# Splitting a vector multiplication, and replanning the first products, in a fast matrix-multiplication kernel

## The chip, the core and the metric

The kernel runs on one core of one Trainium2 chip. The metric is the time on the device in microseconds, as the median of several runs. Five engines matter here: PE (TensorE, the matrix multiplier) with its weight loads, DVE (VectorE), ACT (ScalarE), POOL (GpSimd) and SP (SyncE). POOL and SP mainly issue transfers (DMA) here.

## The reference

```python
x:  16 x 512 x 1024 float32     w1, w2: 1024 x 768 float32
y1 = np.matmul(x, w1)
y2 = np.matmul(x, w2)
return (np.tanh(y1) * y2).astype(np.float32)
```

So 8192 rows of x are multiplied with 1536 columns, and the two halves of the result are joined row by row.

## The kernel before

**Rows and columns.** The rows are cut into 64 row tiles of 128. The contraction length 1024 is cut into 8 blocks of 128 (`KO`), in two halves of four (`KH`). The 1536 columns are cut into three blocks of 512: block a is columns 0 to 511 of w1, block b is columns 0 to 511 of w2, and block g holds the last 256 columns of both. So `tanh(a) * b` gives the first 512 output columns of a row tile (`o`, 128x768), and one half of g times the tanh of the other half gives the last 256.

**Plain part.** The first four row tiles (`HEAD`) are multiplied directly, slice by slice as the weights land: a slices, then g slices, then b slices (lines 420 to 434).

**Triples.** The other 60 row tiles are worked through in 20 triples of three row tiles. A triple is a product of a 3x2 block matrix (three row tiles by two halves of the contraction) with a 2x3 one (two halves by a, b, g). Eighteen block products would be needed; a Strassen-like scheme does it with 15, called p0 to p14 in the list `C_OPS`. Each is four matmuls of 128x512 into one of the 8 PSUM banks (line 443). For it VectorE forms sums of transposed x blocks (`A_SUMS`, named S3, S15 and so on, line 411) and once sums of weight blocks (`B_SUMS`, named B5, B27 and so on, line 402). The products are put together by copies on ScalarE (line 447), which also seed banks that PE then adds to, and by additions on VectorE (line 453; add4, add60 and so on). A triple ends with a tanh on ScalarE for each row tile and column part (line 456; `t` for 512 columns, `th` for 256) and a multiplication on VectorE (line 461; `m` for 512 columns, `mh` for 256). In names like `p6.0` below, the number behind the point is the triple. p6 multiplies the x sum S15, p1 the sum S3, p0 reads the weight sum B27.

**Getting x in.** Row tiles 4, 5 and 6 (the first triple, loaded in the order 6, 4, 5) come by DMA from POOL (line 352), are transposed by PE (line 370), and are evacuated by ScalarE (line 356). Later row tiles are loaded the same way and transposed by DMA from SP (line 377). The b slices are loaded from POOL (line 349), behind one instruction, `gate` (line 483), that waits for the cast of slice g0; the x rows follow them.

**The order.** Nothing runs in an order chosen on the chip: a planner in the kernel's Python (`Planner`) simulates the five engines with given costs, landing times and due times, and writes out the order in which every engine executes. PE's products have a fixed sequence (`PE_ORDER`, with `FIRST_ORDER` for triple 0 and `LAST_ORDER` for the last triple). What the planner gives out is an order alone; on the chip every instruction waits for what it needs, in its place in its engine's queue. So a changed cost or landing time in the plan changes which instruction stands ahead of which, and which bank it uses.

The assumed landings of the first loads (`lands`) grow by a fixed step for each load, and from `LAG_FROM` on all are put later by `LAG`. The casts from float32 to float16 of the a slices are planned on VectorE, those of the g slices on ScalarE (`CAST`).

Row tile 3 has its b part multiplied at the very end, as fillers of 256 columns between the last products (`FILLERS`).

Of the kernel before, what the change touches and what calls it, by code (L numbers as in the profile page):

```python
# [66 lines left out]
)  # L67

PE_ORDER = "7 0+ 13+ 6 10 4+ 5+ 9 12 1 14 3+ 2+ 11 8"
FIRST_ORDER = "10 7 1 6 12 9 11 14 8"  # L70
LAST_ORDER = "0 5 4 13 14 3 2"
FILLERS = "p0", "p3"

# [1 line left out]
class Planner:  # L75
# [9 lines left out]
    def op(self, name, engines, due, needs, fn, *args, behind=(), issued=(), chains=(), xfer=0.0, latency=None, seeds=False,  # L85
           lands=None, hold=0.0):
        assert name not in self.ops, name
        self.ops[name] = dict(engines=engines, due=due, needs=[n for n in needs if n], behind=[n for n in behind if n], issued=[n for n in issued if n], fn=fn, args=args,
                              chains=chains, xfer=xfer, latency=latency, seeds=seeds, lands=lands, hold=hold)
        for c in chains:  # L90
            self.chains.setdefault(c, {"left": 0, "bank": None, "end": 0.0, "act": 0.0, "dve": 0.0})["left"] += 1
# [135 lines left out]
def kernel(  # L227
# [15 lines left out]
    G = N - F  # L243
    HEAD = 4
    TRIPLES = (MT - HEAD) // 3
# [58 lines left out]
    op = plan.op  # L304
# [179 lines left out]

    MM = 0.2158
    SLOT = KH * MM
    CAST = {"a": {"dve": 0.37}, "g": {"act": 0.495}}
    FINE = (5, 36, 37, 45)
    START = 28.6
    ORIGIN = START - 6 * SLOT  # L490
# [2 lines left out]
    for n, entry in enumerate(PE_ORDER.split()):  # L493
        for i in range(TRIPLES):
            position["p" + entry.rstrip("+"), i] = (i + (entry[-1] == "+")) * 15 + n
    for n, p in enumerate(FIRST_ORDER.split()):
        position["p" + p, 0] = 6 + n
# [4 lines left out]
    plan.strict = [f"{p}.{i}" for _, i, p in sequence]  # L502

    XX = 1.4
    LAG_FROM, LAG = 23.0, 1.2
    on_sp = "x00 x10 x20 x30 x01 x11 a4 a5 x21 a6 x31 a7".split() + [f"g{k}{t}" for k in range(KH) for t in range(2)]
    late = [f"b{k}" for s, k in slices if s == "b"]
    rows_in = (HEAD + 2, HEAD, HEAD + 1)
# [11 lines left out]
    for n, what in enumerate(on_sp):  # L520
# [3 lines left out]
        else:  # L524
            s, k = what[0], int(what[1])
# [11 lines left out]
    landed = {}  # L537
    for s, k in slices:
        loads = [f"g{k % KH}{t}" for t in range(2)] if s == "g" else [f"{s}{k}"]
        landed[s, k] = max(lands[n] for n in loads)  # L540
        if s != "b":
            op(f"c{s}{k}", CAST[s], landed[s, k] + 0.3, [f"L{n}" for n in loads], cast_w, s, k)
    all_casts = [f"c{s}{k}" for s, k in slices if s != "b"]
    for t in range(2):
        for k in range(KO):
# [35 lines left out]
    outs = {mt: [] for mt in range(MT)}  # L581

    def reuse_out(mt):
        return [f"st{mt - O_BUFS}"] if mt >= HEAD + O_BUFS else []
# [16 lines left out]
    for n, s in enumerate("agb"):  # L601
        for mt in range(HEAD):
            if (s, mt) == ("b", HEAD - 1):
                continue
            due, behind = (lambda n: landed[slices["agb".index(s) * KO + n]] + 0.8 + 0.02 * mt), []
            finals(mt, s, due(KO - 1) + (5.0, 3.0, 7.0)["agb".index(s)], plain(mt, s, due, behind))

    mt = HEAD - 1
# [31 lines left out]
    def w_needs(v, ks=slice(0, KH)):  # L640
        if v in wsum:
            return [f"B{v}.{p.start}" for p in parts(v) if p.start < ks.stop and ks.start < p.stop]
        bit = v.bit_length() - 1
        return [f"c{s}{bit // 3 * KH + k}" for s in "abg"[bit % 3] for k in range(ks.start, ks.stop)]
# [5 lines left out]
    def x_needs(i, v):  # L650
        if v & (v - 1):
            return [f"S{v}.{i}"]
        bit = v.bit_length() - 1
        mt = HEAD + 3 * i + bit // 2
        return [f"e{mt}{bit % 2}"] if mt < BY_PE else [f"T{mt}"]
# [7 lines left out]
    def needed(i, v):  # L663
        return min([slot_of[i, o[0]] for o in C_OPS if o[1] == "p" and o[4] == v] + [needed(i, u) - 0.5 for u, a, b, _ in A_SUMS if v in (a, b)])

    for i in range(TRIPLES):
        for name, kind, needs, *_ in C_OPS:
            soonest[i, name] = max([until[i, n] for n in needs] + ([slot_of[i, name]] if kind == "p" else []))
            until[i, name] = soonest[i, name] + TIME[kind] + 0.2
        for v, a, b, how in A_SUMS:  # L670
            op(f"S{v}.{i}", {"dve": 0.335}, None, x_needs(i, a) + x_needs(i, b), x_sum, i, v, a, b, how,
               hold=needed(i, v) - S_AHEAD if i > 1 else 0.0,
               behind=[f"{r}.{i - S_BUFS}" for r in a_readers[v]] if i >= S_BUFS else first_done)
            for u in (a, b):
                if not u & (u - 1):
                    xt_readers[HEAD + 3 * i + (u.bit_length() - 1) // 2].append(f"S{v}.{i}")
        for o in C_OPS:
            name, kind, needs = o[:3]
            needs = [f"{n}.{i}" for n in needs]
            chains = sorted({(i, p) for p in o[3:6] if isinstance(p, str) and p[0] == "c"})  # L680
            if kind == "p":
                needs += x_needs(i, o[4]) + w_needs(o[5])
                op(f"{name}.{i}", {"pe": SLOT}, slot_of[i, name], needs, product, i, *o[3:], chains=chains,
                   behind=[f"m{HEAD - 1}y0{KO - 1}"] if (name, i) == ("p3", TRIPLES - 1) else [])
                if not o[4] & (o[4] - 1):
                    xt_readers[HEAD + 3 * i + (o[4].bit_length() - 1) // 2].append(f"{name}.{i}")
                continue
            if kind in ("seed", "copy", "add"):
                before = []
                if o[3][0] == "s":  # L690
                    before = [f"{r}.{i - C_BUFS}" for r in readers[o[3]]] if i >= C_BUFS else all_casts
                if kind == "add":
                    op(f"{name}.{i}", {"dve": 0.6}, None, needs, c_add, i, *o[3:], behind=before, chains=chains, seeds=True)
                else:
                    op(f"{name}.{i}", {"act": 0.495}, None, needs, c_copy, i, *o[3:], behind=before, chains=chains, seeds=True)
                continue
            r = o[3]
            mt = HEAD + 3 * i + r
            due = soonest[i, name] + LAST
            if kind in ("t", "th"):  # L700
                lo, n = (0, F) if kind == "t" else (F, G)
                op(f"{name}.{i}", {"act": 0.5 if n == F else 0.285}, due, needs, c_tanh, i, r, o[4], lo, n, o[5],
                   behind=reuse_out(mt) + ([f"{FIRST_READER[name]}.{i}"] if i == TRIPLES - 1 and name in FIRST_READER else []), chains=chains)
            else:
                lo, n, at = (0, F, 0) if kind == "m" else (F, G, G)
                op(f"{name}.{i}", {"dve": 0.6 if n == F else 0.335}, due + 1, needs, c_mul, i, r, o[4], lo, n, at, chains=chains)
                outs[mt].insert(0 if kind == "m" else 1, f"{name}.{i}")
    for mt in range(MT):
        i = (mt - HEAD) // 3 if mt >= HEAD else -1
# [23 lines left out]
    for mt in range(HEAD, MT):  # L733
        i, r = divmod(mt - HEAD, 3)
# [16 lines left out]
    for n in sorted(soon, key=lambda n: plan.start_of[n]):  # L751
        o = plan.ops[n]
# [3 lines left out]
    for n in order:  # L756
        if n not in soon:
            o = plan.ops[n]
# [102 lines left out]
```

## Time and profile before

| what | value |
|---|---|
| median of 3 runs | 299.58 us (299.41 to 299.83) |
| the profiled execution | 299.71 us |
| its span, first to last instruction | 297.9 us |
| granted TensorE clock, mean | 0.998 |
| instructions on PE, DVE, ACT, POOL | 1374, 539, 454, 129 |

The profile is of one execution. A row of the timeline gives start, duration, engine, line, operation, output and inputs with their shapes, the count of equal instructions in a row, and in brackets the idle time of the engine ahead of it with what ended it. The duration of a merged row reaches from the first start to the last end; instructions of an engine overlap a little, so that two that follow each other start closer together than one lasts. A row of the waits gives engine, tile and line, what it waited for, and then the total in us, the count and the longest. In the groups by line, the count is followed by busy time in us and the mean of one in ns.

### The profile page before, as it was taken

The page shows a single profiled execution, that of the slowest core. Times are in us where ns is not written, and L with a number is a line of the kernel's source. Part 1 is how long each engine was busy: PE and PEld are TensorE (multiplying, and loading weights), DVE is VectorE, ACT ScalarE, POOL GpSimd, SP SyncE. Part 2 cuts the span into 40 slices and gives each one's busy share as a digit, 9 for nine tenths or more (in the row PEclk, how much of TensorE's full clock was granted, in tenths as well). Part 3 has the DMA queues.
Part 4 walks back from the last instruction along what each step waited for, and adds up shares of the span by engine and source line. Part 5 has one row for each costly group of instructions (what it writes and reads, how often), then busy time and mean ns, then how long its engine had stood idle before and what let it go on. Part 6 is the DMA issues. An engine that isn't in the chain of part 4 may idle for free. (4 is left out here: it accounts for less than half of the span.)

```text
span 297.9 us, 4666 instructions
## 1 busy us (share of the span) xinstructions
PE 290.2 (97%) x1374; PEld 132.4 (44%) x1374; DVE 256.4 (86%) x539; ACT 227.2 (76%) x454; POOL 49.6 (17%) x129
## 2 busy tenths in 40 slices
PE   8999999999999999999999999999999999999993
PEld 3444444444444444444444444444444444444441
DVE  1679999989999998988989898898989989898883
ACT  2596799699978979798797988768677776868450
POOL 0073033121212111221110211111111100000000
PEclk9999999999999999999999999999999999999999
DMA  6999999999999999999999999999999989041234
GB/s 233 384 300 203 165 164 153 220 197 262 226 290 231 261 210 235 257 163 249 209 258 143 284 262 157 191 253 297 194 219 228 258 249 296 3 161 54 106 141 162
DMA packets 84427, 63.51 MB, mean 213 GB/s; under 512 B 62768, under 2 KB 66608, under 8 KB 84400
## 3 DMA queue, kind: packets, MB, share of 16 engines
q1 hardware_dynamic: 73600, 44.84, 62.3%
q0 software_dynamic: 9792, 16.78, 35.5%
q10 hardware_dynamic: 1008, 1.57, 1.5%
q8 instruction: 11, 0.18, 0.3%
q14 instruction: 16, 0.13, 0.1%
HBM read 39.85 MB, written 25.17 MB: 218 GB/s over the span
## 5 line engine op out<-in xcount | busy, mean ns | idle before, releaser
L443 PE MATMUL bank<-b,early_x 128*128 128x512 f16 x640 | 148.3, 379 | 0.6 <-DVE early_x L411 0.6
L443 PEld LDWEIGHTS <-early_x 128*128 128x128 f16 x800 | 78.0, 98 | 95.6 <-DVE early_x L411 1.4
L453 DVE TENSOR_TENSOR bank<-bank,arena 128x512 f32<-128x512 f32 x100 | 69.7, 697 | 15.7 <-ACT arena L447 10.0
L447 ACT ACTIVATE arena<-bank 128x512 f32<-128x512 f32 x100 | 59.5, 597 | 29.6 <-PE bank L443 29.2
L461 DVE TENSOR_TENSOR o<-o,bank 128x256 f32<-128x256 f32 (+1 forms) x120 | 63.6, 549 | 5.9 <-ACT o L456 5.3
L380 ACT ACTIVATE junk<-xh 128x1024 f16<-128x1024 f16 x60 | 63.4, 1057 | 0.2
L443 PEld LDWEIGHTS <-xT 128*128 128x128 f16 x400 | 39.0, 98 | 46.5
L443 PE MATMUL bank<-b,xT 128*128 128x512 f16 x240 | 58.3, 379 | 0.0
L456 ACT ACTIVATE o<-bank 128x256 f32<-128x256 f32 (+1 forms) x80 | 34.6, 438 | 15.1 <-DVE bank L453 11.0
L443 PE MATMUL bank<-wh,xT 128*128 128x512 f16 x160 | 41.1, 379 | 0.0
L443 PE MATMUL bank<-wh,early_x 128*128 128x512 f16 x160 | 40.9, 379 | 0.0
L352 POOL DMA_DIRECT2D xh<-in_x_dram x60 | 31.9, 532 | 40.2 <-ACT o L456 24.8
L480 POOL CAST held<-xT 128x1 f32<-128x1 f16 x54 | 12.5, 232 | 135.0 <-DMA xT<-xh 134.9
L411 DVE TENSOR_TENSOR early_x<-early_x,xT 128x512 f16<-128x512 f16 x80 | 33.1, 419 | 0.5
L447 ACT ACTIVATE bank<-bank 128x512 f32<-128x512 f32 x40 | 21.5, 575 | 7.2 <-DVE bank L453 6.1
L456 ACT ACTIVATE o<-arena 128x512 f32<-128x512 f32 x40 | 25.1, 627 | 1.4 <-DVE arena L453 1.4
L420 PE MATMUL bank<-wh,xT 128*128 128x512 f16 x72 | 18.4, 379 | 0.4 <-DVE wh L358 0.3
L411 DVE TENSOR_TENSOR early_x<-xT,xT 128x512 f16<-128x512 f16 x40 | 16.8, 421 | 0.0
L411 DVE TENSOR_TENSOR early_x<-xT,early_x 128x512 f16<-128x512 f16 x40 | 16.8, 420 | 0.0
L453 DVE TENSOR_TENSOR bank<-arena,bank 128x512 f32<-128x512 f32 x20 | 13.9, 695 | 2.4 <-ACT o L456 0.7
L453 DVE TENSOR_TENSOR arena<-bank,arena 128x512 f32<-128x512 f32 x20 | 13.7, 684 | 0.1
L380 ACT ACTIVATE junk<-wh 128x768 f16<-128x768 f16 x16 | 13.5, 844 | 0.2
(47 smaller groups left out, 137.0 us busy)
## 6 DMA issues: line engine op xcount, KB each, us to landing
out_dram<-o SPq DMA_DIRECT2D x60, 384.0 KB, 5.4
xh<-in_x_dram POOLq DMA_DIRECT2D x60, 256.0 KB, 6.1
arena<-in_w_dram SPq DMA_DIRECT2D x12, 256.0 KB, 5.4
early_x<-in_x_dram SPq DMA_DIRECT2D x8, 256.0 KB, 5.2
arena<-in_w_dram ACTq DMA_DIRECT2D x4, 256.0 KB, 5.9
wh<-in_w_dram POOLq DMA_DIRECT2D x8, 128.0 KB, 5.3
xT<-xh SPq DMA_TRANSPOSE x57, 6.6
out_dram<-o SPq DMA_DIRECT2D x4, 128.0 KB, 2.6
```

Of the source, the lines that this page charges most:

```text
L352: pin(nc.gpsimd.dma_start(xh(mt), xf[mt]))
L380: pin(nc.scalar.activation(junk[:, :src.shape[-1]], src, ACT.Abs, scale=scale, accum_out=sums[:, column:column + 1]))
L411: pin(engine[e].tensor_tensor(x_operand(i, v), x_operand(i, a), x_operand(i, b), OP[how]))
L420: pin(nc.tensor.matmul(bank(chain)[:, :rhs.shape[-1]], xt(mt)[:, k, :], rhs, start=first, stop=k == KO - 1, skip_group_check=True))
L443: pin(nc.tensor.matmul(place(i, dst), x_operand(i, a)[:, k, :], w_rhs(b, k), start=begins and k == 0, stop=k == KH - 1, skip_group_check=T ...
L447: pin(nc.scalar.activation(place(i, dst), place(i, src), ACT.Copy, scale=float(sign)))
L453: pin(nc.vector.tensor_tensor(place(i, dst), a, b, ALU.add if signs == (1, 1) else ALU.subtract))
L456: pin(nc.scalar.activation(out_tile(HEAD + 3 * i + r)[:, lo:lo + n], place(i, src)[:, :n], ACT.Tanh, scale=float(sign)))
L461: pin(nc.vector.tensor_tensor(o, o, place(i, src)[:, at:at + n], ALU.mult))
L480: pin(nc.gpsimd.tensor_copy(held, xt(mt)[:, 0, :1]))
```

## The change

There are four edits:

1. In the triples 0 to 18 the 512-column multiplication `m` becomes two of 256 columns, `mx` and `my`, each an operation of its own for the planner, with a planned cost of 0.335 each in place of 0.6. In the last triple it stays whole.
2. `LAG_FROM` goes from 23.0 to 21.5: the plan takes loads as late from the second b slice on.
3. p7 and p10 of triple 0 change places, so that p7 comes first.
4. The cast of slice g0 goes from ScalarE to VectorE. `gate` waits for this cast.

```diff
-FIRST_ORDER = "10 7 1 6 12 9 11 14 8"
+FIRST_ORDER = "7 10 1 6 12 9 11 14 8"
...
-    CAST = {"a": {"dve": 0.37}, "g": {"act": 0.495}}
+    CAST = {"a": {"dve": 0.37}, "g": {"act": 0.495}, "g0": {"dve": 0.37}}
...
-    LAG_FROM, LAG = 23.0, 1.2
+    LAG_FROM, LAG = 21.5, 1.2
...
-            op(f"c{s}{k}", CAST[s], landed[s, k] + 0.3, [f"L{n}" for n in loads], cast_w, s, k)
+            op(f"c{s}{k}", CAST.get(f"{s}{k}", CAST[s]), landed[s, k] + 0.3, [f"L{n}" for n in loads], cast_w, s, k)
...
+            elif kind == "m" and i < TRIPLES - 1:
+                for t in range(2):
+                    op(f"{name}{'xy'[t]}.{i}", {"dve": 0.335}, due + 1, needs, c_mul, i, r, o[4], t * G, G, t * G, chains=chains)
+                    outs[mt].append(f"{name}{'xy'[t]}.{i}")
             else:
                 lo, n, at = (0, F, 0) if kind == "m" else (F, G, G)
                 op(f"{name}.{i}", {"dve": 0.6 if n == F else 0.335}, due + 1, needs, c_mul, i, r, o[4], lo, n, at, chains=chains)
```

Since the planner works everything out anew, the order on every engine but SP and POOL changes in many places, and so do the banks. The ones that the text below speaks of: on VectorE, B6 goes behind the first halves of B24, B18 and B26, the first half of B27 goes from ahead of S3 of triple 0 to behind S21 of triple 1, S3 of triple 2 goes ahead of S21 and S51 of triple 1, and mh1 of triple 0 goes ahead of add4 of triple 0. On PE, five of the first eight fillers go ahead of p5 and p4 of the last triple.

## The prediction

> **What bounds the kernel now.** I read the page first, then PE's own waits, then the timeline of each engine over the first 54 us and the last 14, because these two hold nearly all the time that PE loses.
>
> ```profile
> span 297.9 us, 4666 instructions
> ...
> PE 290.2 (97%) x1374; PEld 132.4 (44%) x1374; DVE 256.4 (86%) x539; ACT 227.2 (76%) x454; POOL 49.6 (17%) x129
> ...
> 17.00:34.00 17.00, 16.29 (x92) 7.62 (x90) 15.93 (x37) 14.10 (x30) 7.78 (x15) 1.00 1.10 217
> ...
> 52.00:150.00 98.00, 98.00 (x456) 44.43 (x454) 89.78 (x187) 82.63 (x168) 19.70 (x53) 1.00 1.17 233
> ...
> PE bank L443 <- DVE early_x L411: 0.6, 1, 0.6
> ...
> PE bank L370 <- DMA xh<-in_x_dram: 0.2, 1, 0.2
> ```
>
> The rows that begin with a stretch (17 to 34 us, 52 to 150 us) give the busy time of PE, of its weight loads, of VectorE, ScalarE and POOL, then the granted clock, the busy share of DMA and GB/s; the last two rows are PE's longest single wait after the start and a smaller one. From 52 to 150 us PE is busy 98.00 of 98.00 us. PE is the bound, at the full granted clock (1.00), with one product of four matmuls every 0.863 us (52.32 and 53.18 below are 0.86 apart). It never waits between 38 and 284 us. So time can be won in three places alone: at the first g block, around the first products, and in the last triple. Anything else can only lose.
>
> The stretch around the first products, PE first:
>
> ```profile
> 16.83 1.46 PE L420 MATMUL bank<-wh,xT 128*128 128x512 f16 x6
> ...
> 29.71 0.62 PE L370 MATMUL bank<-ident_h,xh 128*128 128x128 f16 x8 [0.17 <-DMA xh<-in_x_dram]
> 30.17 1.03 PE L443 MATMUL bank<-wh,xT 128*128 128x512 f16 x4
> ...
> 31.49 1.03 PE L443 MATMUL bank<-wh,xT 128*128 128x512 f16 x4
> 32.43 1.04 PE L443 MATMUL bank<-b,early_x 128*128 128x512 f16 x4
> 34.01 3.76 PE L443 MATMUL bank<-b,early_x 128*128 128x512 f16 x16 [0.55 <-DVE early_x L411]
> ...
> 52.32 1.03 PE L443 MATMUL bank<-wh,xT 128*128 128x512 f16 x4
> 53.18 1.03 PE L443 MATMUL bank<-b,xT 128*128 128x512 f16 x4
> ```
>
> p10 starts at 30.17, p7 at 31.49, p1 at 32.43, p6 at 34.01. A product every 0.863 us would put p6 at 33.29, so p6 is 0.72 late, for an x sum (S15) that VectorE makes. The vector side of it:
>
> ```profile
> 23.66 0.69 DVE L402 TENSOR_TENSOR b<-wh 128x1024 f16<-128x1024 f16 x1 [0.67 <-DMA wh<-in_w_dram]
> ...
> 30.13 1.90 DVE L402 TENSOR_TENSOR b<-b,b 128x1024 f16<-128x1024 f16 x3
> 31.94 0.43 DVE L411 TENSOR_TENSOR early_x<-xT 128x512 f16<-128x512 f16 x1
> ...
> 32.74 1.22 DVE L411 TENSOR_TENSOR early_x<-early_x,xT 128x512 f16<-128x512 f16 x3
> ...
> 36.61 0.43 DVE L411 TENSOR_TENSOR early_x<-xT 128x512 f16<-128x512 f16 x1 [0.45 <-DMA xT<-xh]
> ...
> 48.42 0.43 DVE L411 TENSOR_TENSOR early_x<-xT 128x512 f16<-128x512 f16 x1 [0.17 <-DMA xT<-xh]
> ...
> 49.42 0.88 DVE L411 TENSOR_TENSOR early_x<-early_x,xT 128x512 f16<-128x512 f16 x2
> ...
> 50.74 0.70 DVE L453 TENSOR_TENSOR bank<-arena,bank 128x512 f32<-128x512 f32 x1
> ...
> 30.15 1.07 ACT L356 COPY xT<-bank 128x512 f16<-128x512 f16 x2 [0.36 <-PE bank L370]
> 31.46 1.07 ACT L356 COPY xT<-bank 128x512 f16<-128x512 f16 x2 [0.24 <-PE bank L370]
> ```
>
> Read it as a queue in order: VectorE waits 0.67 for a b slice at 23.66 (the weight sum B6), is then busy with weight sums to 32.03, and only then makes S3, S34, S35, S11, S15, the last ending at 33.96 (32.74 + 1.22). At 36.61 and 48.42 it waits again, for transposed row tiles 7 and 10.
>
> **The change part by part.** Places in the new order come from listing both programs' instructions by engine.
>
> g0 cast by VectorE. ScalarE's cast begins at 16.16 and VectorE stands idle until 16.81:
>
> ```profile
> 14.60 0.43 DVE L358 CAST wh<-arena 128x512 f16<-128x512 f32 x1 [0.24 <-DMA arena<-in_w_dram]
> ...
> 16.81 0.95 DVE L402 TENSOR_TENSOR b<-wh 128x512 f16<-128x512 f16 x2 [1.79 <-ACT wh L356]
> ...
> 16.16 1.14 ACT L356 CAST wh<-arena 128x512 f16<-128x512 f32 x2
> ...
> 23.68 2.75 POOL L352 DMA_DIRECT2D xh<-in_x_dram x5 [1.55 <-DMA wh<-in_w_dram]
> ```
>
> The two ScalarE casts take 1.14 together, so one is about 0.6; VectorE's takes 0.43 from about the same start and ends near 16.6. PE's first g matmul (16.83) and the gate ahead of the b loads come about 0.2 earlier. Neither reaches the end: the row transpose of 29.71 waits for its x row by DMA, and POOL issues that row at 23.68 when a b slice has landed, not when the gate opens. PE waits 0.4 there in place of 0.17: gain nothing, as long as the x rows land when they did; with the row loads following the gate it would be 0.2.
>
> Late loads in the plan. It changes no transfer, only the order on VectorE: B6 goes behind three other weight sums whose slices are there, so the 0.67 goes, and one half of the sum B27 (0.6, a third of the 1.90 row) moves from before S3 to after 36.61. VectorE would be free for S3 1.27 earlier, at 30.67, but S3 reads tile 4, evacuated at 31.22 (30.15 + 1.07). S3 then starts at 31.28; S11 reads tile 5, evacuated at 32.53 (31.46 + 1.07), so it starts at 32.59; S11 and S15 take 0.88 (the pair at 49.42), so S15 ends at 33.47 and p6 starts at 33.52: 0.49 earlier than 34.01. The limit is now the x row of tile 5.
>
> p7 first. p7 and p10 read the two halves of tile 6, both evacuated before 30.17, and both are four matmuls: they change places at no cost. The copy that reads p7 stands behind the evacuations that end at 32.53 either way; the sum that reads p10, now done at 32.52, stands behind S15.
>
> The halves. 57 multiplications (19 triples of 3) become 114:
>
> ```profile
> L461 DVE TENSOR_TENSOR o<-o,bank 128x512 f32<-128x512 f32 x60 | 40.0, 681 | 0.6 <-ACT o L456 0.3 <-DMA out_dram<-o 0.2
> ...
> L461 DVE TENSOR_TENSOR o<-o,bank 128x256 f32<-128x256 f32 x60 | 24.8, 417 | 5.3 <-ACT o L456 5.0
> ...
> 24.27 0.75 DVE L427 TENSOR_TENSOR o<-o,bank 128x256 f32<-128x256 f32 x2
> ...
> 42.98 0.68 DVE L461 TENSOR_TENSOR o<-o,bank 128x512 f32<-128x512 f32 x1
> 43.58 0.69 DVE L453 TENSOR_TENSOR bank<-bank,arena 128x512 f32<-128x512 f32 x1
> ```
>
> Two halves in a row start 0.33 apart (0.75 less 0.417), so they hold the queue 0.66, against 0.60 for the whole (42.98 to 43.58): 0.06 each, 3.4 us in all, out of some 41 us in which VectorE is idle. By durations alone it would be 0.153 each (2 x 0.417 less 0.681), 8.7 us. [...] By either price PE's steady stretch has room, and no bank is released sooner. I take 0.06.
>
> Where the 0.49 goes. From 36.61 on VectorE has no idle time but the wait at 48.42 until past 51, and both ends of that stretch are landings of transposes, which do not come sooner because PE does. In the new order two things stand in it that did not: half of B27 (0.6) and two split multiplications (0.12); against that two x sums (0.67) move behind the wait at 48.42. So VectorE arrives there as before and waits as before. Behind the wait stand those two x sums (0.67) and one half-width multiplication (0.33) ahead of add4, less 0.4 of waits between dependent steps that they fill: add4 starts at 51.36 rather than 50.74 and ends at 52.05. Product p7 of triple 2 takes its bank: not before 52.10, 0.22 sooner than 52.32. A tanh on ScalarE reads add4, and the copy behind it frees what p0 of triple 1 needs:
>
> ```profile
> 51.47 0.39 ACT L456 ACTIVATE o<-bank 128x256 f32<-128x256 f32 x1
> 51.75 0.59 ACT L447 ACTIVATE arena<-bank 128x512 f32<-128x512 f32 x1
> ...
> 40.74 0.53 POOL L352 DMA_DIRECT2D xh<-in_x_dram x1 [0.79 <-ACT junk L380]
> ...
> DMA to landing us min/median/max: 3.1/6.6/10.1
> ```
>
> Tanh at 52.11, copy 0.28 later at 52.39 to 52.98, p0 at 53.04: 0.14 sooner than 53.18. That is what is left if tile 10 lands at the same time. With durations as the price of the halves it would be nothing. If the tile lands sooner, since a row load ahead of it waits for ScalarE's row sums (40.74), which follow PE, up to 0.4 is kept. Between 0.14 and 0.4 I take 0.2, nearer to the landing that is measured.
>
> The last triple. The rows are PE's and one of ScalarE's:
>
> ```profile
> 285.55 1.94 PE L443 MATMUL bank<-b,early_x 128*128 128x512 f16 x8
> ...
> 288.89 0.58 ACT L447 ACTIVATE bank<-bank 128x512 f32<-128x512 f32 x1 [0.77 <-DVE bank L453]
> ...
> 289.92 1.89 PE L443 MATMUL bank<-b,xT 128*128 128x512 f16 x8
> ```
>
> The new order puts five of the eight 256-column matmuls of row tile 3 between p0, p5 and p4 (p5 and p4 are the row at 285.55), and one half-width multiplication ahead of add60, which p4 needs. That makes p4 later by its 0.33 or a little more, and the copy that ends at 289.47 with it, to 289.8. p3 reads this copy; now it starts at 289.92, 0.45 after it, with all eight matmuls ahead of it, and then with three of them, right behind the copy: 289.85 to 290.0. I take nothing, 0.1 on either side.
>
> **The sum.** 0.2 less than the profiled 299.71 (span 297.9, 1.8 around it). The median of the runs, 299.58, lies 0.13 below that run, so 299.4. A measurement of this kernel can tell about 0.2%, 0.6 us.
>
> **The rivals.** Faster, the rows come sooner: tiles 4 and 5 and the transposes behind them land up to 0.8 earlier because the b loads start earlier. For it: PE and S11 wait for exactly these rows. Against it: DMA is busy throughout (busy share 1.10 in the table of stretches for 17 to 34 us), so an earlier start moves no bytes sooner. Then VectorE bounds p6 near 33.1, and everything behind it moves along: some 0.9 won, 298.7. I give it and smaller forms that pass 0.6 a chance of 0.32.
>
> Slower, the late tile: S3 of triple 2 now stands ahead of two ready sums, so a late tile 10 stops VectorE with work behind it, and PE with it, since p0 follows that landing by 4.6 us. It decides from a landing 0.14 later than now; at 0.75 later it costs 0.6. For it: transposes land after 3.1 to 10.1 us (row above), so a change in what flies beside them can move one by that much. Against it: the loads ahead come no later than now. Price 0.7: 300.3. Chance 0.23.
>
> Forecast, within 0.6 us of now: 0.45. The range takes in the faster rival to 298.7 and nearly all of the slower one, 300.2; the forecast's own is 299.1 to 299.8.
>
> **What would show it.** Right: the first g matmul near 16.6; no wait at B6; p6 near 33.5; VectorE's wait for tile 10 still ending near 48.4; then PE waits by about 0.2 at p7 of triple 2 and p0 of triple 1. Wrong: p6 still at 34.0 (then the x rows or VectorE's order are not what I think); no PE wait near 52 with p6 earlier (then the gain is kept, 0.4 or more); any PE wait between 60 and 280 (then the halves cost latency that I left out).

## The result, and the profile after

The changed kernel takes 298.61 us (median of 6 runs, 298.32 to 298.88), the kernel before, run beside it, 299.59 (6 runs, 299.41 to 300.41). The ratio is 0.9962, with a 95% interval from 0.9949 to 0.9976. So it is faster by about 1 us, where the forecast was 0.2 and the lower end of the range was 298.7.

The page of the changed kernel (the profiled execution took 298.88), its first lines and its instruction queues:

```profile
span 297.1 us, 4747 instructions
...
PE 290.1 (98%) x1374; PEld 132.4 (45%) x1374; DVE 259.7 (87%) x597; ACT 226.3 (76%) x453; POOL 50.4 (17%) x129
...
q8 instruction: 11, 0.18, 0.3%
q14 instruction: 17, 0.14, 0.2%
```

PE's busy time is the same to 0.1 us and the span is 0.8 shorter. VectorE has 58 instructions more: 57 multiplications and one cast. The last two rows are the loads of the program itself, which the page counts with the packets of the 16 DMA engines, as it does the data. In the trace they are packets of 16 KB (q8) and 8 KB (q14). There is one more of the latter than in the row of the kernel before:

```profile
q14 instruction: 16, 0.13, 0.1%
```

PE's timeline of the changed kernel, the rows that answer to those shown of before:

```profile
29.18 0.61 PE L370 MATMUL bank<-ident_h,xh 128*128 128x128 f16 x8
29.62 1.03 PE L443 MATMUL bank<-wh,xT 128*128 128x512 f16 x4
30.49 0.61 PE L370 MATMUL bank<-ident_h,xh 128*128 128x128 f16 x8
...
32.96 1.25 PE L443 MATMUL bank<-b,early_x 128*128 128x512 f16 x5
...
51.86 1.02 PE L443 MATMUL bank<-wh,xT 128*128 128x512 f16 x4 [0.44 <-DVE bank L453]
52.72 1.03 PE L443 MATMUL bank<-b,xT 128*128 128x512 f16 x4
```

p6 of triple 0 starts at 32.96 in place of 34.01. At p7 of triple 2 PE waits 0.44 for add4, and 0.46 of the 1.05 is left (51.86 against 52.32, 52.72 against 53.18). VectorE's timeline shows why:

```profile
29.35 1.29 DVE L402 TENSOR_TENSOR b<-b,b 128x1024 f16<-128x1024 f16 x2
30.81 0.43 DVE L411 TENSOR_TENSOR early_x<-xT 128x512 f16<-128x512 f16 x1 [0.17 <-ACT xT L356]
...
31.60 1.30 DVE L411 TENSOR_TENSOR early_x<-early_x,xT 128x512 f16<-128x512 f16 x3
...
48.08 0.43 DVE L411 TENSOR_TENSOR early_x<-xT 128x512 f16<-128x512 f16 x1 [0.50 <-DMA xT<-xh]
...
51.02 0.69 DVE L453 TENSOR_TENSOR bank<-arena,bank 128x512 f32<-128x512 f32 x1
```

Two half sums of weights stand ahead of S3 (30.81), where the kernel before had three. VectorE waits for the transposed tile 10 until 48.08, 0.34 sooner than before but for longer, and add4 (51.02) comes behind. From there PE loses 0.13 once more ahead of p0 of triple 2 (65.80) and 0.12 in the last triple. Its last matmul is the last of three in this row of the kernel before:

```profile
292.19 0.49 PE L420 MATMUL bank<-wh,xT_kept 128*128 128x256 f16 x3
```

and in this one of the changed kernel:

```profile
291.97 0.49 PE L420 MATMUL bank<-wh,xT_kept 128*128 128x256 f16 x3
```

A row's last start is its start and its duration less 0.27, which the last matmul lasts: 292.41 before and 292.19 now (292.414 and 292.186 in the traces).

**So PE ends only 0.23 sooner, and the span is 0.76 shorter (297.86 and 297.10 in the traces). The other 0.53 lies behind PE's last matmul.** (The medians lie 0.98 apart; for the 0.2 that is left the two profiled executions show nothing.) Behind the last matmul VectorE's last multiplication follows at the same distance in both (0.76), and so does the issue of SP's last store (1.20: rows 293.62 and 293.39). What differs is how long that store takes. The DMA view from just ahead of its issue to the end, of the kernel before (columns: queue, packets, MB, share; then the issue, its KB and us to landing):

```profile
q14 instruction: 2, 0.02, 0.7%
...
out_dram<-o SPq DMA_DIRECT2D x1, 128.0 KB, 3.2
```

and of the changed kernel:

```profile
q14 instruction: 2, 0.02, 0.8%
...
out_dram<-o SPq DMA_DIRECT2D x1, 128.0 KB, 2.6
```

The traces have 16 landings for each store, one for each of its parts, and it counts as landed with the last. By them 15 parts land 3.4 us after the start of PE's last matmul in both kernels (295.82 and 295.58). The sixteenth lands 0.95 later before (296.77), and 0.44 later in the changed kernel (296.02). Beside the store the trace has an 8 KB packet of instructions, the first of the two in the view: it starts at 295.21 before, amid the store, and five of the store's 1 KB packets behind it, from 295.56 to 296.01, last 88 to 152 ns in place of 46. In the changed kernel it starts at 295.37, right behind the store's data (the last 1 KB packet starts at 295.32).

### The profile page after: what moved, and what is told of

It is laid out like the page before. It is cut to its first block, busy times and chain, and to the rows that moved or that the text cites. A ratio compares the mean times of both kernels' runs of the same rounds, so it can differ in the third digit from the quotient of the medians.

```text
span 297.1 us, 4747 instructions
## 1 busy us (share of the span) xinstructions
PE 290.1 (98%) x1374; PEld 132.4 (45%) x1374; DVE 259.7 (87%) x597; ACT 226.3 (76%) x453; POOL 50.4 (17%) x129
## 5 line engine op out<-in xcount | busy, mean ns | idle before, releaser
L461 DVE TENSOR_TENSOR o<-o,bank 128x256 f32<-128x256 f32 (+1 forms) x177 | 68.1, 420 | 6.5 <-ACT o L456 5.7
L480 POOL CAST held<-xT 128x1 f32<-128x1 f16 x54 | 13.6, 252 | 137.8 <-DMA xT<-xh 137.7
L453 DVE TENSOR_TENSOR arena<-arena,bank 128x512 f32<-128x512 f32 x20 | 13.6, 682 | 0.0
```

The lines of the kernel that those rows point to most:

```text
L453: pin(nc.vector.tensor_tensor(place(i, dst), a, b, ALU.add if signs == (1, 1) else ALU.subtract))
L461: pin(nc.vector.tensor_tensor(o, o, place(i, src)[:, at:at + n], ALU.mult))
L480: pin(nc.gpsimd.tensor_copy(held, xt(mt)[:, 0, :1]))
```

## The experiments

Two theories of the 0.53 stood against each other: **fetch** (instructions that are loaded beside the last store hold up one of its parts; the split makes VectorE's program longer and shifts the loads) and **order** (the split changes the order of the last triple and with it the spacing of the last stores). For the front of the kernel it was **rows** (x rows come sooner because the gate opens sooner) against **order** on VectorE; **end** in the first expectations means that the last store landed sooner by chance. In the expectations "the start of PE's last group" is the start of its last matmul. Four comparisons were made, each with its own runs of the kernel before: medians 299.59, 299.51 (e1 to e4), 299.46 (e5 to e7) and 299.44 (e9 to e12).

**The first g slice back on ScalarE** (e1_no_g).

```diff
-    CAST = {"a": {"dve": 0.37}, "g": {"act": 0.495}, "g0": {"dve": 0.37}}
+    CAST = {"a": {"dve": 0.37}, "g": {"act": 0.495}}
```

> The change without its fourth edit: g0 is cast by ScalarE again, so the gate opens near 16.8 instead of 16.6. Theory 'rows' (the earlier gate lets the x rows of tiles 4 and 5 land 0.7 sooner, and the rest follows): the rows land as before (tile 4's transpose near 29.7, p6 no sooner than 33.5) and at least 0.7 of the 1.0 us gained is lost, time 299.3 or more. Theory 'order' (VectorE's new order by the later planned loads is what gains): it keeps 0.7 or more of the 1.0, time 298.9 or less. Theory 'end' (the last store lands sooner by luck of that run): time anywhere from 298.6 to 299.6 with the landing of the last store spread as widely as before in some runs.

Measured: 299.32, ratio 1.0 (0.9978 to 1.0022). The number is that of "rows", the mechanism is not: the x rows of tiles 4 and 5 land at 29.04 and 30.36, as soon as with the edit, though the cast of slice g0 ends 0.35 later (17.01 against 16.66 in e4). What changed is the plan. VectorE's timeline of this kernel:

```profile
29.72 2.49 DVE L402 TENSOR_TENSOR b<-b,b 128x1024 f16<-128x1024 f16 x4
32.13 0.41 DVE L411 TENSOR_TENSOR early_x<-xT 128x512 f16<-128x512 f16 x1
```

Four half sums of weights stand ahead of S3, where the changed kernel has two (1.29 from 29.35), and S3 starts at 32.13 in place of 30.81. PE also gets tile 4's transpose later (30.46). p6 starts at 33.95. So this small cast decides how much the late loads bring, through the planner.

**The late loads undone** (e2_no_lag).

```diff
-    LAG_FROM, LAG = 21.5, 1.2
+    LAG_FROM, LAG = 23.0, 1.2
```

> The change without its second edit: the plan has the loads late from 23.0 on as before. Theory 'rows': the x rows land as in the changed kernel (transpose of tile 4 near 29.2), VectorE again waits for the b slice ahead of B6 near 23.7, p6 near 33.6, and 0.5 to 0.7 of the gain stays: 298.9 to 299.1. Theory 'order': most of the gain goes, 299.3 or more.

Measured: 299.09, ratio 0.9984 (0.9963 to 1.0005); p6 at 33.63. The wait ahead of B6 is back, and three half sums stand ahead of S3 (1.89 from 29.76):

```profile
23.61 0.69 DVE L402 TENSOR_TENSOR b<-wh 128x1024 f16<-128x1024 f16 x1 [0.63 <-DMA wh<-in_w_dram]
```

These are the numbers that "rows" expected. The medians of this kernel and the changed one (e4) differ by 0.39 and p6 by 0.55, but the intervals of the two ratios overlap. The profiled execution of this kernel took 300.21, 1.1 over its median, and PE lost 1.1 in it at 242.93.

**The multiplications whole again** (e3_no_split): the branch for `mx` and `my` taken out.

> The change without its first edit: the 512-column multiplications stay whole. Theories 'rows' and 'order' alike: the same as the changed kernel within 0.2 us, since the multiplications are hidden under PE, or 0.1 better for 3.4 us less of VectorE. A rival, that the halves gain by themselves: 0.4 us or more slower than the changed kernel.

Measured: 299.16, ratio 0.9989 (0.997 to 1.0007): 0.46 slower than the changed kernel in the same comparison (e4), though the two intervals overlap. That was the rival's case. But PE ends earlier without the split: its last matmul starts at 291.83, against 292.05 in e4 and 292.19 in the changed kernel. The 15 parts of the last store land at 295.22, and the sixteenth at 296.33. Against e4 the split with its order costs PE 0.22 (p7 of triple 2 starts at 51.74 here and at 51.73 there, so the landing of tile 10 is no part of it), and it gains more behind PE: the span ends 4.92 after the last matmul's start there, and 5.58 here.

**The changed kernel once more** (e4_all_again).

> The changed kernel once more, for a second profile. Theory 'rows': tile 4's transpose starts near 29.2 again, p6 near 32.7, time 298.6. Theory 'end': the rows or the last store's landing differ from the first profile by 0.4 or more while the time is the same 298.6, so that they can't be the cause.

Measured: 298.70, ratio 0.9965 (0.9947 to 0.9983). p6 starts at 33.08, and the last store lands 3.83 after the start of the last matmul, to the hundredth as in the first profile. The end is not chance.

**The split alone** (e5_only_split): the kernel before with edit 1 and nothing else.

> The kernel before with the split multiplications alone. Theory 'fetch' (the end of the kernel is set by one DMA engine that carries an 8 KB instruction fetch beside the last store; 57 more VectorE instructions move that fetch out of the end): PE's last product ends no sooner than before, within 0.2 us, but the last store lands 3.83 us after the start of PE's last group, as in every kernel with the split so far, against 4.36 and 4.50 in the two without; time 299.1, 0.4 to 0.5 less than before. Rival 'order' (the last triple's new order spaces out the last stores, instruction fetches have no part in it): the same 3.83, the same time; the two are told apart by the padded kernels. Rival 'sum' (the parts of the change only work together): time as before, 299.5, and 4.4 us after the last group.

Measured: 299.15, ratio 0.9984 (0.9974 to 0.9995). PE's last matmul starts at 292.47, 0.06 later than before, and the store lands 3.83 behind it. A real gain of 0.3 without any on PE.

**Sixteen memsets, nothing else** (e6_pad16). They write a spare column in VectorE's idle time ahead of its first cast (1.93 us in all) and compute nothing.

```diff
     pin(nc.vector.tensor_copy(ident_h, ident))
+    for _ in range(16):
+        pin(nc.vector.memset(spare, 0.0))
```

> The kernel before, every multiplication whole, with 16 one-column memsets of a spare tile on VectorE ahead of its first cast. They compute nothing. Theory 'fetch': the 8 KB fetch that began at 295.21 falls some 16 VectorE instructions sooner, near 287, ahead of the last stores; the last store lands about 3.8 us after the start of PE's last group in place of 4.36, and the time is 0.4 to 0.5 under the kernel before, 299.05. Rival 'order': nothing of the last triple has changed, so 4.4 us and 299.5, or up to 0.2 more for the memsets in the head.

Measured: 298.81, ratio 0.9975 (0.9963 to 0.9987). Sixteen useless instructions make the kernel faster by 0.65. The DMA view from just ahead of SP's last store to the end:

```profile
q14 instruction: 1, 0.01, 0.7%
...
out_dram<-o SPq DMA_DIRECT2D x1, 128.0 KB, 2.2
```

One 8 KB packet is left there, behind the store (296.68, the store landed at 296.48); the other now starts at 287.58 in place of 295.21. The last triple is as before, so "order" falls: the last store is held up by an instruction load, and VectorE's program length decides when this comes.

**Late loads, p7 first, g slice, and the memsets** (e7_lpg_pad16): edits 2 to 4 with the 16 memsets, the multiplications whole.

> The late loads, p7 first and the first g slice on VectorE, the multiplications whole, and the 16 memsets. Theory 'fetch': PE ends as in the kernel without the split (291.83 in its profile, 0.36 sooner than in the changed kernel), and the last store follows after 3.8 us instead of 4.50: 298.3 to 298.5, faster than the changed kernel by 0.2 to 0.4 and than the kernel before by 1.0 to 1.2. Rival 'order': 299.1, as without the memsets.

Measured: 298.02, ratio 0.9955 (0.9942 to 0.9968); once more with other runs beside it (e12_best_again):

> The kernel of the 16 memsets once more, beside the others: 298.0, the last store 3.39 us after the start of PE's last group, and p7 of triple 2 near 51.3 if tile 10's transpose lands ahead of 47, near 51.8 if it lands near 48 as in the changed kernel.

298.03, ratio 0.9951 (0.9932 to 0.9971). It is the fastest of all, 1.4 under the kernel before and 0.6 under the changed one. PE's timeline of the first of the two:

```profile
33.01 1.25 PE L444 MATMUL bank<-b,early_x 128*128 128x512 f16 x5
...
51.31 1.03 PE L444 MATMUL bank<-wh,xT 128*128 128x512 f16 x4
52.17 1.03 PE L444 MATMUL bank<-b,xT 128*128 128x512 f16 x4
```

There is no wait at p7 of triple 2: here tile 10's transpose lands at 46.10 (46.29 in e12), and the 1.0 won at p6 is kept whole. The last matmul starts at 291.41, the store lands 3.39 later.

**The kernel before, a second profile** (e8_before_again).

> The kernel before once more, for a second profile. If the late landing of the x rows of tiles 4 and 5 (29.67 and 30.91 us) belongs to this kernel's plan, it is there again within 0.15 us; if it was one execution's, the rows land near 29.0 and 30.4, as in all four kernels run since. Theory 'fetch': an 8 KB fetch near 295.2 and the last store 4.3 to 4.5 us after the start of PE's last group.

Measured: one run of 301.0. The rows land at 29.12 and 30.44, so the late rows that the prediction saw (29.67 and 30.91) were that one execution's; yet p6 starts at the old time. PE's timeline:

```profile
29.38 0.61 PE L370 MATMUL bank<-ident_h,xh 128*128 128x128 f16 x8
...
33.96 3.76 PE L443 MATMUL bank<-b,early_x 128*128 128x512 f16 x16 [0.55 <-DVE early_x L411]
...
53.62 1.02 PE L443 MATMUL bank<-wh,xT 128*128 128x512 f16 x4 [1.20 <-ACT o L456]
```

In the kernel before, p6 hangs on VectorE's order alone, not on the rows. And PE loses 1.3 at p7 of triple 2, because the transposed tiles 10 and 11 land at 48.70 and 51.05, in place of 48.40 and 49.23. At the end the packet starts 2.79 after the last matmul's start, and the store lands after 4.35.

**The fetch put back, and moved away again** (e9_lpg_pad128, e10_lpg_pad144): e7 with more memsets, most of them behind the whole multiplications. (The head has 14 of them and `m` is 8 in e9; 15 and 13 in e10.) The expectations count 128 and 144 memsets. The traces have 152 and 168, and 24 waits for semaphores fewer on VectorE, so that in all the programs are longer than e3's by 128 and 144 instructions (4664 in e3, 4792 and 4808 on the pages). The 128 instructions of one 8 KB packet are an estimate in the expectation; in the trace of before, two of the 8 KB packets (242.60 and 295.21) start 125 VectorE instructions apart.

```diff
         pin(nc.vector.tensor_tensor(o, o, place(i, src)[:, at:at + n], ALU.mult))
+        for _ in range((3 if i < m else 2) if n == F and i < TRIPLES - 1 else 0):
+            pin(nc.vector.memset(spare, 0.0))
```

> The kernel of the 16 memsets (late loads, p7 first, first g slice on VectorE, multiplications whole) with 128 of them: 14 in the head and two or three behind each whole multiplication. They compute nothing. One 8 KB fetch is 128 instructions if one takes 64 bytes, so 128 more put VectorE's last fetch back where it was without any. Theory 'fetch': a fetch some 2.7 us after the start of PE's last group, beside the last store, which lands 4.4 us after that start in place of 3.39; about 0.5 slower than the kernel of 144, and 0.5 slower than that of 16 or somewhat more, since the memsets take VectorE's time. Rival 'order': no difference between 128 and 144.

> The same with 144 memsets: 15 in the head and two or three behind each multiplication. Theory 'fetch': the last fetch falls some 8 us ahead of the end as with 16, the last store lands 3.4 us after the start of PE's last group, and the time is about 0.5 under that of the kernel with 128, although it has 16 instructions more; against the kernel with 16 it stands within 0.3. Rival 'order': as with 128, or slower by the 16 memsets.

Measured: 300.21, ratio 1.0042 (1.0015 to 1.0068), and 300.05, ratio 1.0015 (1.0004 to 1.0026). The same DMA view, of e9:

```profile
q14 instruction: 2, 0.02, 1.0%
...
out_dram<-o SPq DMA_DIRECT2D x1, 128.0 KB, 3.3
```

and of e10:

```profile
q14 instruction: 1, 0.01, 0.9%
...
out_dram<-o SPq DMA_DIRECT2D x1, 128.0 KB, 2.2
```

The place of the load is as "fetch" said: with 128 more instructions it is back beside the store (2.74 after the last matmul's start, as without memsets), with 16 more again it is 5.54 ahead. The times missed: both are 2 us slower than with 16 memsets, and only 0.16 apart. In the profiles PE's last matmul starts at 292.47 in e9 and at 293.86 in e10, in place of 291.41 in e7, and this covers the price of the load. PE's waits at its products come to 0.2 in e9 and 0.8 in e10; that the many memsets in VectorE's queue are what delays PE is the author's estimate.

**p10 first again** (e11_lg_pad16): e7 without edit 3.

> The kernel of the 16 memsets without p7 first: late loads and the first g slice on VectorE, p10 first in triple 0. By the prediction, which took the swap for free: within 0.2 us of the kernel with it, p6 of triple 0 near 33.0. Rival: the planner builds another order around it, and p6 falls to 33.5 or later, 298.5 or more.

Measured: 298.57, ratio 0.9979 (0.9958 to 1.0); p6 at 33.27, 0.26 later than with p7 first, and tile 10's transpose at 48.02 with a wait of 0.25 at p7 of triple 2. The median is the rival's, p6 lies between the two. The swap was not free in the plan: it is worth 0.26 at p6. The rest of the 0.54 goes with the transpose's landing, which differs.

**All ends side by side**, from the traces (us; the packet is the last 8 KB packet but one, its start counted from that of PE's last matmul; the last one starts 3.58 to 3.62 after it, 3.81 in e1):

| kernel | last matmul starts | 8 KB packet | store landed after | span ends after |
|---|---|---|---|---|
| before, and again (e8) | 292.41, 293.72 | +2.80, +2.79 | 4.36, 4.35 | 5.44, 5.43 |
| whole, edits 2 to 4 (e3) | 291.83 | +2.74 | 4.50 | 5.58 |
| the same, 152 memsets (e9) | 292.47 | +2.74 | 4.49 | 5.58 |
| changed, and again (e4) | 292.19, 292.05 | +3.18, +3.18 | 3.83, 3.83 | 4.91, 4.92 |
| changed without the g cast (e1) | 292.62 | +3.18 | 3.82 | 4.90 |
| changed without late loads (e2) | 293.42 | +3.18 | 3.83 | 4.91 |
| split alone (e5) | 292.47 | +3.18 | 3.83 | 4.92 |
| before and 16 memsets (e6) | 293.08 | -5.50 | 3.40 | 4.69 |
| e7, and again (e12) | 291.41, 291.40 | -5.55, -5.54 | 3.39, 3.40 | 4.68, 4.69 |
| e7 with p10 first (e11) | 291.92 | -5.49 | 3.40 | 4.68 |
| 168 memsets (e10) | 293.86 | -5.54 | 3.39 | 4.70 |

Three ends, by the place of one packet: 5.4 to 5.6, 4.9 and 4.7. The profiled executions of e6 and e8 lost time at the transposes, which is why their PE ends late; the end behind it does not depend on that.

## Why the prediction was wrong

The step that failed is the one in the sum: "0.2 less than the profiled 299.71 (span 297.9, 1.8 around it)". It carried PE's gain to the end unchanged and gave the split no gain anywhere ("I take 0.06"). The split wins PE nothing, but it makes VectorE's program longer by 57 multiplications, and with the split alone (e5) as with the whole change the end behind PE's last matmul went from 5.44 to 4.9: a term of 0.5 that the sum put at nothing without a reason. Neither the forecast nor a rival had that term. The faster rival's 298.7 lies near the result, but not by its mechanism.

Point by point:

- *PE bounds, and only the head, the first products and the last triple can win.* Right for PE. Between 60 and 280 us no wait of PE shows but the 0.13 ahead of 65.80. The second profile (e4) has it too (65.66); e3 with the multiplications whole has not, but the split alone (e5) has not either, so it belongs to the order of this plan and not to the halves as such.
- *The g slice.* The first g matmul was forecast near 16.6, as PE's earlier start, and the cast ends at 16.54. "Gain nothing" was wrong in the plan: without it p6 comes at 33.95, since the planner then puts two more half sums ahead of S3.
- *Late loads, p6 at 33.52.* B6's wait went and half of B27 moved, as forecast, and p6 came at 32.96. "The limit is now the x row of tile 5" rested on landings that one execution had; in the thirteen other profiles they came 0.4 to 0.7 sooner. The faster rival had the landings right, and its cause (b loads that start earlier) wrong: they are as early in the second profile of before.
- *p7 first, no cost.* No cost, and 0.26 won at p6.
- *The halves, 0.06 each.* In the windows from 52 to 150 us the changed kernel's VectorE has 24 instructions and 1.59 us more than before, 0.066 each:

```profile
52.00:150.00 98.00, 98.00 (x455) 44.34 (x454) 91.37 (x211) 83.11 (x171) 20.25 (x52) 1.00 1.16 229
```

  By durations it would have been 0.153 each (2 x 0.417 less 0.681); the measurement decides for the distance of starts.
- *Most of the gain lost at tile 10.* Right, and the best part of the forecast: VectorE's wait ended at 48.08 (forecast 48.4), p7 came at 51.86 (52.10), p0 at 52.72 (53.04), and PE's end 0.23 sooner (0.2). That last agreement is in part luck: p0 came 0.46 sooner, more than the 0.14 to 0.2 of the forecast, since the tile landed 0.34 sooner, and the two later losses of 0.13 and 0.12, which the forecast did not have, took half of it away. The slower rival's case is real too, but before as well as after: the second profile of before paid 1.3 there.
- *The last triple, nothing within 0.1.* PE lost 0.12 there; without the split it lost nothing (p0 to the last matmul 7.83 in e3, 7.95 changed).

What stays open: why tile 10's transpose lands at 46.1 to 46.3 in e7 and e12 and between 47.4 and 48.7 in the other twelve profiles, and which engine's program the packet at +3.18 in the split kernels belongs to. It is probably not VectorE's. Before, two of the 8 KB packets start at VectorE's 581st and 706th instruction of 709, waits counted (242.60 and 295.21); in the changed kernel two start at its 579th and 701st of 772 (222.11 and 266.77), so VectorE's own load seems to have moved 28 us ahead of the stores. SP's program is 16 instructions longer with the split, because of added waits at its stores, and the packet at +3.18 starts at SP's 314th instruction in all split kernels; the programs with whole multiplications have only 313 on SP. No run took this apart, so the step from the split to the packet's new place is in part argued; that the packet's place sets the end is what the memsets show.

## What to carry to other kernels

Count a kernel's time as the end of the bound engine plus the tail behind it, and look in the tail for packets of the instruction queues: an edit that changes the number of instructions moves them (16 memsets moved one from 2.80 behind the start of the last matmul to 5.50 ahead of it), and a store is done only with the last of its 16 parts, which such a packet can hold up (0.95 us here). A landing time taken from one profile is one draw; where a step hangs on it, a second execution of the same kernel is worth more than a finer argument. Where a planner writes the order, undoing one edit makes another plan, so read the new order before a difference is put down to the edit.

## What the runs showed of the hardware

In these traces the program is loaded during the run, and a load can slow the data beside it (in the kernel before, five 1 KB packets of the last store took 88 to 152 ns in place of 46). In the kernel before there are 11 packets of 16 KB, each about 0.9 to 1.8 us long, and 16 of 8 KB, mostly 0.31 us; the page has all loads under q8 (16 KB) and q14 (8 KB). Adding 128 instructions to VectorE put its load back in the same place (+2.74 in e3 and e9), so 8 KB are 128 instructions there, 64 bytes each. Beside the last store a load cost 0.75 us of the span (5.44 behind the last matmul's start before, 4.69 in e6).
